# Down projection of an encoder's FFN: seven block products in place of eight, activation operands split ahead and kept in DRAM

## Chip, cores and metric

One core of one Trainium2 chip runs the whole layer in one launch. The metric is device time in microseconds, from launch to the last instruction; three runs of the kernel before took 1522.60, 1526.57 and 1527.08 us. Engines are named as the profile names them: PE is TensorE (PEld its weight loads), DVE is VectorE, ACT is ScalarE, POOL is GpSimd, SP is SyncE.

## What is computed

One layer of a bidirectional encoder over 1024 tokens of width 1024, in float32. The token mixer (a convolution branch and a gated spatial branch, merged) ends in a residual sum; then comes the FFN with DFF = 2816, and a last RMSNorm. The change lies in the FFN:

```python
D_FF = ((8 * D_MODEL // 3 + 255) // 256) * 256      # 2816
h2 = rmsnorm(x, norm_ffn[l])
x = x + (jax.nn.silu(h2 @ w_ffn_gate[l]) * (h2 @ w_ffn_up[l])) @ w_ffn_down[l]
return rmsnorm(x, norm_final)
```

## The kernel before

**Precision.** Every large product is made of three matmuls. An operand is split into a rounded half `hi` (type fp32r, written by ACT, line 84) and the remainder `lo` (DVE, line 85); hi·hi, hi·lo and lo·hi are summed in PSUM. One matmul has 128x128 weights (the stationary operand, loaded by PEld) and 512 moving columns.

**Order of the work.** The program is written with a tile framework. It tracks which instruction writes and reads each tile, sets the semaphores, and picks each engine's fixed order of instructions from its own estimate of when each is ready. So a filler matmul can stand between two blocks that wait for another engine. A PSUM tile of two banks counts as one: a write to one half waits for a read of the other.

**Gate and up (lines 562 to 701).** The 22 row blocks f of DFF go in pairs, f = 2, 4, ..., 20 (0 and 1 are done in the plain way, `plain`, line 564). For a pair, `blocks` (line 653) forms the 2x2 block product of weights and activations with seven products instead of eight; they are numbered 1, 2, 6, 5, 7, 3, 4 in the order in which they run. A product is `block`, 12 matmuls. Sums of weight blocks are made and split in `w_operands` (line 610). Products accumulate into the PSUM halves b1, b2 (tile pa) and b3 (tile pb); between them ACT copies a partial sum out (lines 662, 666, 668) and DVE subtracts it (lines 664, 670, 672). First the gate's seven products run, then the up's; DVE multiplies the two, line 693 and, for the block that ends last, line 696. The product, a tile pair `fa`, is written to DRAM tensors `ff_d` by a DMA that POOL issues (line 700).

**Down (lines 704 to 771).** The output is 8 token tiles of 128 by 1024 columns. It is made in two halves h of four token tiles, each with its four full PSUM tiles. For each of 22 f, SP loads the half's activations (`load_ff`, 256 KB, split into hi and lo) and the weight rows (`load_wd`, 512 KB, split; the last twelve f are kept split for the second half). Per f and token tile run 3 x 2 matmuls, two column halves with the same weights in PE:

```python
for l, r in ((lh, wh), (lh, wl), (ll, wh)):
    for c in cols:
        nc.tensor.matmul(p[c], l[:, sl], r[:, c * H:(c + 1) * H], ...)
```

The last eight f (from `LAST`) are held back and run tile by tile, so that `finish` (line 723) of one tile runs beside the matmuls of the next: DVE adds the residual (732), ACT squares (733), DVE scales by the norm's weights (739), POOL takes the power (741), DVE and ACT scale (745, 747), SP stores.

**Memory.** Pool `act` has 42 buffers of 4 KB a partition, `ws` (raw weights) 3, `wh` (split weights) 4.

Of the kernel before, what the change touches and what calls it, by code (L numbers as in the profile page):

```python
# [32 lines left out]
def encoder_kernel(ctx, tc, x, w_in, w_v, vecs, w_conv_out, sgu_b, w_sp, b_sp,  # L33
                   w_sgu_out, w_o, w_gate, w_up, w_down, norm_final, out):
    nc = tc.nc
# [211 lines left out]
    wg = wnext(0)  # L247
# [7 lines left out]
    pg, pv = PS("pg_0"), PS("pv_0")  # L255
# [249 lines left out]
    def two(name, dt=F32):  # L505
        return A(name, dt, (P, 2, H))
# [52 lines left out]
            h2_transpose(0, (2, 3))  # L559


    ff_d = [dram.tile([P, S], F32, name=f"ff_d{f}") for f in range(NF)]

    def plain(p, w, h):

# [21 lines left out]
    h2_transpose(1, (2, 3))  # L587
    plain(pg, wg, 1)
    plain(pu, wu, 1)
    glu_pair(0, pg, pu)  # L590
    wg = wnext()
    pg = PS("fg_1")
    for h in range(2):
# [6 lines left out]
        plain(pu, wu, h)  # L600
    h2_sums(2)
    h2_sums(3)
    glu_pair(1, pg, pu)

    def w_raw(src, name):
        w = wp.tile([P, D], F32, tag="ws", name=f"ws_{name}", bufs=3)
        nc.sync.dma_start(w, src)
        return w

    def w_operands(src, f, name):  # L610


        r0, r1 = w_raw(src[f], f"{name}{f}"), w_raw(src[f + 1], f"{name}{f + 1}")
        x11, x12, x21, x22 = r0[:, :H], r0[:, H:], r1[:, :H], r1[:, H:]
        sa, sb = two(f"sa_{name}{f}"), two(f"sb_{name}{f}")
        sp, sq, sr, sz = sa[:, 0, :], sa[:, 1, :], sb[:, 0, :], sb[:, 1, :]
        out = {}

        def put(n, s):
            if n in (6, 7, 3):  # L620
                o = two(f"w{n}_{name}{f}", F32R)
            else:
                o = wp.tile([P, 2, H], F32R, tag="wh", name=f"w{n}_{name}{f}", bufs=4)
# [18 lines left out]
        return out  # L642
# [33 lines left out]
    def ffn_in(f, wg, next_w):  # L676
        a = [two(f"fa_{f + n}") for n in range(2)]

        def gate_block(n, h):
            def put(add):  # L680
                add(a[n][:, h, :])
                nc.scalar.activation(a[n][:, h, :], a[n][:, h, :], AF.Silu)
            return put
        blocks(wg, f"g{f}", gate_block(0, 0),
               lambda b: nc.scalar.activation(a[1][:, 0, :], b, AF.Silu),
               gate_block(1, 1), gate_block(0, 1))
        wu = w_operands(w_up, f, "u")
        u = T(f"u_{f}", (P, 2, H))

        def up_block(n, h, i):  # L690
            def put(add):
                add(u[:, i, :])
                nc.vector.tensor_mul(a[n][:, h, :], a[n][:, h, :], u[:, i, :])
            return put
        blocks(wu, f"u{f}", up_block(0, 0, 0),
               lambda b: nc.vector.tensor_mul(a[1][:, 0, :], a[1][:, 0, :], b),
               up_block(1, 1, 1), up_block(0, 1, 0))
        wn = next_w()
        for n in range(2):
            nc.gpsimd.dma_start(ff_d[f + n], a[n].rearrange("p a b -> p (a b)"))  # L700
        return wn


    KEEP = 10
    LAST = 14
    kept = {}

    def load_wd(f):
        if f in kept:
            return kept[f]  # L710
        w = load_split(w_down[f * P:(f + 1) * P, :], f"d{f}", pool=act if f >= KEEP else None)
# [11 lines left out]
    def finish(t, p):

        x2 = A(f"x2b_{t}")
        nc.gpsimd.dma_start(x2, x2_d[t])
        o = A(f"o_{t}")
        ss = small.tile([P, 2], F32, tag="ss2", name=f"ss2_{t}")
        v = small.tile([P, 1], F32, tag="ms", name=f"ms_f{t}")
        for c in range(2):  # L730
            cs = slice(c * H, (c + 1) * H)
            nc.vector.tensor_add(x2[:, cs], x2[:, cs], p[c])  # L732
            nc.scalar.activation(o[:, cs], x2[:, cs], AF.Square, scale=D ** -0.5,
                                 accum_out=ss[:, c:c + 1])
            if c == 0:
                nc.vector.tensor_scalar(ss[:, 0:1], ss[:, 0:1], EPS, None, ALU.add)
            else:
                nc.vector.tensor_add(v, ss[:, 1:2], ss[:, 0:1])
            nc.vector.tensor_mul(x2[:, cs], x2[:, cs], nf[:, cs])
        r = small.tile([P, 1], F32, tag="rstd", name=f"rstd_f{t}")  # L740
        nc.gpsimd.tensor_tensor(r, v, nhalf[:, 0:1], op=ALU.pow)
        for c in range(2):
            cs = slice(c * H, (c + 1) * H)
            if c == 0:
                nc.vector.tensor_scalar(o[:, cs], x2[:, cs], r, None, ALU.mult)
            else:
                nc.scalar.activation(o[:, cs], x2[:, cs], AF.Copy, scale=r)
            nc.sync.dma_start(out[t * P:(t + 1) * P, cs], o[:, cs])

    wg = w_operands(w_gate, 2, "g")  # L750
    for f in range(2, NF, 2):
        wg = ffn_in(f, wg, lambda: w_operands(w_gate, f + 2, "g") if f + 2 < NF else None)

    nf = A("nf_bc")
    nc.gpsimd.dma_start(nf, norm_final.to_broadcast([P, D]))
    for h in range(2):
        p = [PS(f"fd_{4 * h + t}") for t in range(4)]
        tail = {}
        for f in range(NF):
            ffs, wd = load_ff(f, h), load_wd(f)  # L760
            if f >= LAST:
                tail[f] = ffs, wd
                continue
            for t in range(4):
                tm_mm(halves(p[t]), ffs, wd, slice(t * P, (t + 1) * P), f == 0, False)
        for t in range(4):
            for c in range(2):
                for f, (ffs, wd) in tail.items():
                    tm_mm(halves(p[t]), ffs, wd, slice(t * P, (t + 1) * P), False,
                          f == NF - 1, (c,))  # L770
            finish(4 * h + t, halves(p[t]))
# [60 lines left out]
```

## Time and profile before

| | us |
|---|---|
| median of three runs (lowest to highest) | 1526.57 (1522.60 to 1527.08) |
| the profiled execution's own time | 1524.07 |
| its span, first to last instruction | 1522.3 |
| PE busy | 1497.1 |
| DVE busy | 901.1 |
| ACT busy | 441.5 |
| POOL busy | 68.0 |

The span is cut by the views into stretches: the mixer until about 835, gate and up until 1270, the down projection until 1512, and the end. A busy PE says that a matmul was in it; whether PE ran without a hole is told by the chain of waits and by what the engines waited for. Granted clock 1.00 means 2.4 GHz.

### The profile page before, as it was taken

What the parts mean: (1) busy time and instruction counts of PE and PEld (TensorE: products, weight loads), DVE (VectorE), ACT (ScalarE), POOL (GpSimd) and SP (SyncE); (2) the same over time, 40 slices, a digit from 0 to 9 for tenths busy, and PEclk for the clock granted to TensorE, in tenths of its full rate; (3) what the DMA queues carried; (4) which work ended last, traced back from release to release, by engine and by line L of the source; (5) the groups of instructions that cost most, each with busy time, mean ns of one, the idle gap of its engine ahead of it and who ended that gap; (6) DMA issues with size and microseconds to landing.
All of it is one profiled execution on the core that took longest, in us unless ns stands there. A gap on an engine that the chain in (4) does not pass through costs nothing.

```text
span 1522.3 us, 16449 instructions
## 1 busy us (share of the span) xinstructions
PE 1497.1 (98%) x6728; PEld 1233.7 (81%) x6728; DVE 901.1 (59%) x1075; ACT 441.5 (29%) x643; POOL 68.0 (4%) x116
## 2 busy tenths in 40 slices
PE   6999999999999999999999999999999999999997
PEld 6888898888888888888888888888888888887885
DVE  4789699578999815633623665555555554443402
ACT  5221001111111113821313543333333333332401
POOL 1000100000000000010010000000000000000000
PEclk9999999999999999999999999999999999999999
DMA  4250001111112222371431122222222225753402
GB/s 184 59 163 14 1 28 50 47 55 43 58 67 78 75 77 90 110 277 43 152 139 70 56 69 84 84 83 84 84 83 83 81 93 186 223 179 119 172 2 81
DMA packets 43035, 141.73 MB, mean 93 GB/s; under 512 B 4784, under 2 KB 4784, under 8 KB 42960
## 3 DMA queue, kind: packets, MB, share of 16 engines
q1 hardware_dynamic: 32256, 101.73, 20.9%
q0 software_dynamic: 10704, 38.96, 7.1%
q8 instruction: 52, 0.85, 0.2%
q14 instruction: 23, 0.19, 0.0%
HBM read 112.36 MB, written 28.31 MB: 92 GB/s over the span
## 4 chain that ended last, share of the span: by engine, by line
PE 98%; DVE 0%; DMA 0%; ACT 0%; issue 0%; POOL 0%; POOLq 0%; SPq 0%; DVEq 0%; ACTq 0%
PE fd L494 16%; PE pa_u L649 9%; PE pa_g L649 9%; PE pga L110 6%; PE po L494 6%; PE pco L110 6%; PE py L110 6%; PE pb L110 6%; PE pu L110 6%; PE pg L110 6%; PE pv L110 6%; PE pb_u L649 4%; PE pb_g L649 4%; PE v L300 2%; PE v L298 2%; PE v L299 2%
## 5 line engine op out<-in xcount | busy, mean ns | idle before, releaser
L218 DVE SCALAR_TENSOR_TENSOR conv<-c,vec,conv 128x1021 f32<-128x1021 f32 (+14 forms) x240 | 301.3, 1274 | 4.4
L494 PE MATMUL fd<-wh_d,ff 128*128 128x512 f32 x704 | 199.0, 389 | 2.0 <-ACT ff L84 2.0
L494 PEld LDWEIGHTS fd<-wh_d,ff 128*128 128x128 f32 x704 | 132.0, 188 | 29.9 <-ACT ff L84 2.5
L84 ACT CAST wh_in<-ws_in 128x1024 fp32r<-128x1024 f32 x40 | 42.2, 1054 | 303.3 <-PE pg L110 77.5
L494 PE MATMUL fd<-wl_d,ff 128*128 128x512 f32 x352 | 118.8, 389 | 0.0
L649 PE MATMUL pa_g<-t,w_g 128*128 128x512 f32 x360 | 88.7, 395 | 0.0
L649 PE MATMUL pa_u<-t,w_u 128*128 128x512 f32 x360 | 88.7, 395 | 0.0
L649 PEld LDWEIGHTS pa_u<-t,w_u 128*128 128x128 f32 x360 | 66.0, 188 | 18.2 <-DVE u L664 3.1
L649 PEld LDWEIGHTS pa_g<-t,w_g 128*128 128x128 f32 x360 | 66.0, 188 | 18.2 <-DVE fa L664 3.0
L110 PE MATMUL pg<-hT,wh_in 128*128 128x512 f32 (+1 forms) x272 | 75.2, 388 | 3.1 <-ACT hT L180 1.6
L494 PEld LDWEIGHTS fd<-wl_d,ff 128*128 128x128 f32 x352 | 66.1, 188 | 13.7
L85 DVE TENSOR_TENSOR wl_in<-ws_in,wh_in 128x1024 fp32r<-128x1024 f32 x40 | 48.8, 1220 | 41.2 <-ACT wh_in L84 41.1
L110 PE MATMUL pv<-hT,wh_in 128*128 128x512 f32 (+1 forms) x272 | 70.9, 377 | 0.0
L110 PE MATMUL pga<-hT,wh_in 128*128 128x512 f32 x256 | 69.4, 393 | 0.0
L494 PE MATMUL po<-wh_o,mT 128*128 128x512 f32 x256 | 69.1, 390 | 0.0
L110 PE MATMUL pu<-hT,wh_in 128*128 128x512 f32 x256 | 68.4, 389 | 0.0
L110 PE MATMUL py<-gT,wh_so 128*128 128x512 f32 x256 | 68.4, 389 | 0.0
L110 PE MATMUL pco<-sT,wh_co 128*128 128x512 f32 x256 | 68.4, 389 | 0.0
L110 PE MATMUL pb<-hT,wh_in 128*128 128x512 f32 x256 | 68.4, 389 | 0.0
L85 DVE TENSOR_TENSOR wl_d<-ws_d,wh_d 128x1024 fp32r<-128x1024 f32 x32 | 39.1, 1225 | 45.3 <-ACT wh_d L84 45.2
L110 PEld LDWEIGHTS pg<-hT,wh_in 128*128 128x128 f32 x272 | 51.4, 192 | 14.3 <-ACT hT L180 2.4
L732 DVE TENSOR_TENSOR x2b<-x2b,fd 128x512 f32<-128x512 f32 x16 | 10.3, 684 | 82.5 <-PE fd L494 82.5
(220 smaller groups left out, 2697.2 us busy)
## 6 DMA issues: line engine op xcount, KB each, us to landing
ws_in<-in_w_in SPq DMA_DIRECT2D x40, 512.0 KB, 3.7
ws_d<-in_w_down SPq DMA_DIRECT2D x32, 512.0 KB, 4.3
ws_g<-in_w_gate SPq DMA_DIRECT2D x22, 512.0 KB, 3.8
ws_u<-in_w_up SPq DMA_DIRECT2D x22, 512.0 KB, 3.9
ff_d<-fa POOLq DMA_DIRECT2D x22, 512.0 KB, 4.1
ffr<-ff_d SPq DMA_DIRECT2D x44, 256.0 KB, 3.7
x<-in_x SPq DMA_DIRECT2D x16, 512.0 KB, 6.6
ws_v<-in_w_v SPq DMA_DIRECT2D x8, 512.0 KB, 3.8
```

Of the source, the lines that this page charges most:

```text
L84: nc.scalar.copy(hi, src)
L85: nc.vector.tensor_sub(lo, src, hi.bitcast(F32))
L110: nc.tensor.matmul(p[:, h * H + lo_t:h * H + hi_t], wt[:, sl], a[part][h][j][:, i, lo_t:hi_t], start=(k == 0 and wt is hi and part == 0), ...
L218: nc.vector.scalar_tensor_tensor(o[:, a:b], c[:, a + d:b + d], vcol(V_CW, j * TAPS + t), o[:, a:b], ALU.mult, ALU.add)
L298: nc.tensor.matmul(p[:, i2, :], lh, whi, start=(k == 0), stop=False)
L299: nc.tensor.matmul(p[:, i2, :], lh, wlo, start=False, stop=False)
L300: nc.tensor.matmul(p[:, i2, :], ll, whi, start=False, stop=(k == KT - 1))
L494: nc.tensor.matmul(p[c], l[:, sl], r[:, c * H:(c + 1) * H], start=(start and l is lh and r is wh), stop=(stop and l is ll))
L649: nc.tensor.matmul(p, w[n][:, q, sl], a[i][:, r, :], start=(start and i == 0 and m == 0), stop=(i == 3 and m == 2), skip_group_check=True)
L732: nc.vector.tensor_add(x2[:, cs], x2[:, cs], p[c])
```

## The change

- The down projection too becomes a 2x2 block product with seven products. Blocks: the contraction rows 2i and 2i+1 (i = 0 to 10, `NI` = 11), the token halves, and the two column halves of 512. Each product n runs over the 11 i; one step (n, i) is four token tiles by three matmuls. A product's four results lie in two PSUM tiles (`group`).
- The activation operands: blocks 1, 2, 4 of `fa` go to DRAM raw and are split after loading, as before. The four sums (6, 5, 7, 3) are made by DVE beside gate and up, split there (`ff_out`: four adds, four ACT casts, four subtractions for each pair) and written to DRAM as hi and lo together, 512 KB each. POOL issues these stores, and in the down projection the loads, whose destination has type fp32r.
- The weight sums are made in place in the raw tiles `rlo` and `rhi`, and each of 77 weight operands is split just before use (`down_split`). Loads are issued up to five steps ahead of the running one (`LOADS`), splits two steps (`SPLITS`).
- Residual sums, squares and scales are spread over products 7, 3 and 4; four token tiles are stored during product 4 (DMAs issued by ACT), four after it, the last five i being held back (`LAST`).
- `ws` has 6 buffers instead of 3, the norm's weights are loaded before gate and up, and the space that is kept for POOL's DMA descriptors is 4096 bytes a partition.

```diff
-        ws = wp.tile([P, D], F32, tag="ws", name=f"ws_{name}", bufs=3)
+        ws = wp.tile([P, D], F32, tag="ws", name=f"ws_{name}", bufs=6)
...
+    def ff_out(i, a):
+        x11, x21, x12, x22 = a[0][:, 0, :], a[0][:, 1, :], a[1][:, 0, :], a[1][:, 1, :]
+        for n, blk in ((1, x11), (2, x12), (4, x22)):
+            nc.gpsimd.dma_start(ff_d[n][i], blk)
+
+        o = {n: wp.tile([P, 2, H], F32, tag="ws", name=f"ffo{n}_{i}", bufs=6) for n in (5, 6, 7, 3)}
+        nc.vector.tensor_add(o[5][:, 1, :], x21, x22)
+        nc.vector.tensor_add(o[6][:, 1, :], x11, o[5][:, 1, :])
+        nc.vector.tensor_add(o[7][:, 1, :], x11, x21)
+        nc.vector.tensor_add(o[3][:, 1, :], x12, o[6][:, 1, :])
+        for n in (6, 5, 7, 3):
+            hi, lo = o[n][:, 0, :], o[n][:, 1, :]
+            nc.scalar.copy(hi.bitcast(F32R), lo)
+            nc.vector.tensor_sub(lo, lo, hi)
+            nc.gpsimd.dma_start(ffo_d[n][i], o[n])
...
         wn = next_w()
-        for n in range(2):
-            nc.gpsimd.dma_start(ff_d[f + n], a[n].rearrange("p a b -> p (a b)"))
+        ff_out(f // 2, a)
...
+    LAST, LOADS, SPLITS = 6, 6, 2
+    steps = [(n, i) for n in (1, 2, 6, 5, 7, 3, 4) for i in range(NI)]
...
+        if n in ff_d:
+            raw = wp.tile([P, H], F32, tag="ws", name=f"ffr{n}_{i}", bufs=6)
+            nc.sync.dma_start(raw, ff_d[n][i])
+            raws[n, i] = raw
+        else:
+            fos[n, i] = wp.tile([P, 2, H], F32R, tag="ws", name=f"fo{n}_{i}", bufs=6)
+            nc.gpsimd.dma_start(fos[n, i], ffo_d[n][i])
...
+    def down_mm(p, t, ops, start, stop):
+        a, w = ops
+        sl = slice(t * P, (t + 1) * P)
+        for m, (q, r) in enumerate(((0, 0), (0, 1), (1, 0))):
+            nc.tensor.matmul(p, a[:, q, sl], w[:, r, :], start=(start and m == 0),
+                             stop=(stop and m == 2), skip_group_check=True)
...
+    g1 = group("a")
+    down(1, g1, True)
+    g2 = group("b")
+    down(2, g2, True, copies(s1, g1))
+    down(6, g1, False, [lambda t=t, g=g2: nc.vector.tensor_sub(s1[t], g[t], s1[t])
+                        for t in range(4)])
+    g2 = group("c")
+    down(5, g2, True, copies(s2, g1))
+    down(7, g1, False, copies(s5, g2) + [
+        lambda: get_res(range(4, 8)), lambda: less_res(range(4, 8), 1, s5),
+        lambda: get_res(range(4)), lambda: less_res(range(4), 1, s2),
+        lambda: add_res(range(4), 0, s1)])
+    down(3, g2, False, [lambda t=t: add_res([4 + t], 1, [g1[t]]) for t in range(4)])
+    tail = []
+    for i in range(NI):
+        ops = down_operands(4, i)
+        if i < 4:
+            add_res([i], 1, [g2[i]], last=True)
+        elif i < 8:
+            store(i - 4, nc.scalar, 1)
+        if i >= LAST:
+            tail.append(ops)
+            continue
+        for t in range(4):
+            down_mm(g1[t], t, ops, False, False)
+    for t in range(4):
+        for n, ops in enumerate(tail):
+            down_mm(g1[t], t, ops, False, n == len(tail) - 1)
+        add_res([4 + t], 0, [g1[t]], last=True)
+        store(4 + t, nc.sync, 0)
...
+    nc = _bacc.Bacc("TRN2", target_bir_lowering=False, num_devices=1,
+                     dynamic_dma_scratch_size=4096)
```

**Places where the order moves.** First the PE's order in the down projection. Before, for one f and the first two of four token tiles (fd is the tile's PSUM, wh_d and wl_d the split weight rows, ff the split activations; x2 are the two column halves):

```order
L494 MATMUL fd_8354<-wh_d_8365,ff_0_8360 128x512 x2
L494 MATMUL fd_8354<-wl_d_8366,ff_0_8360 128x512 x2
L494 MATMUL fd_8354<-wh_d_8365,ff_0_8360 128x512 x2
L494 MATMUL fd_8355<-wh_d_8365,ff_0_8360 128x512 x2
L494 MATMUL fd_8355<-wl_d_8366,ff_0_8360 128x512 x2
L494 MATMUL fd_8355<-wh_d_8365,ff_0_8360 128x512 x2
```

With the change, the first three steps of product 1 (fd_a: its two PSUM tiles, two token tiles in each; wd and fo: the split operands of the step):

```order
L811 MATMUL fd_a_8682<-wd_0_8644,fo_0_8641 128x512 x6
L811 MATMUL fd_a_8683<-wd_0_8644,fo_0_8641 128x512 x6
L811 MATMUL fd_a_8682<-wd_1_8650,fo_1_8647 128x512 x6
L811 MATMUL fd_a_8683<-wd_1_8650,fo_1_8647 128x512 x6
L811 MATMUL fd_a_8682<-wd_2_8691,fo_2_8688 128x512 x6
L811 MATMUL fd_a_8683<-wd_2_8691,fo_2_8688 128x512 x6
```

A pair of f was 48 matmuls in each token half; a step is 12, and there are 77 steps.

Second, DVE at the start of a pair's gate products, here f = 18. Before, from the last product of the pair before to the subtraction that PE waits for (line 664: fa from pa and ACT's copy s):

```order
L693 TENSOR_TENSOR fa_7331<-fa_7331,u_7462 128x512
L696 TENSOR_TENSOR fa_7332<-fa_7332,pa_u_7463 128x512
L85 TENSOR_TENSOR w_g_7589<-ws_g_7563,w_g_7589 128x512
L627 SCALAR_TENSOR_TENSOR w_u_7700<-ws_u_7694,w_u_7700 128x512
L664 TENSOR_TENSOR fa_7594<-pa_g_7596,s_g_7598 128x512
```

With the change (ffo: the sums of the pair before; line 724 is 696 before, 567 is 627, 690 is 664):

```order
L584 TENSOR_TENSOR ffo_8_8083<-fa_7819,fa_7820 128x512
L724 TENSOR_TENSOR fa_7820<-fa_7820,pa_u_7951 128x512
L85 TENSOR_TENSOR w_g_8077<-ws_g_8051,w_g_8077 128x512
L585 TENSOR_TENSOR ffo_8_8084<-fa_7819,ffo_8_8083 128x512
L586 TENSOR_TENSOR ffo_8_8085<-fa_7819 128x512
L587 TENSOR_TENSOR ffo_8_8086<-fa_7820,ffo_8_8084 128x512
L591 TENSOR_TENSOR ffo_8_8083<-ffo_8_8083 128x512
L591 TENSOR_TENSOR ffo_8_8084<-ffo_8_8084 128x512
L591 TENSOR_TENSOR ffo_8_8085<-ffo_8_8085 128x512
L591 TENSOR_TENSOR ffo_8_8086<-ffo_8_8086 128x512
L567 SCALAR_TENSOR_TENSOR w_u_8209<-ws_u_8203,w_u_8209 128x512
L690 TENSOR_TENSOR fa_8103<-pa_g_8105,s_g_8107 128x512
```

The eight new operations of the pair before stand ahead of line 690 (once line 664).

Third, PE between product 1 and product 6 of the same gate. Before (pb: product 5, taken forward as a filler; pa with y: product 2; pa with t: product 6):

```order
L649 MATMUL pb_g_7597<-t_0_5609,w_g_7578 128x512 x3
L649 MATMUL pb_g_7597<-t_1_5627,w_g_7578 128x512
L649 MATMUL pa_g_7596<-y_0_5181,w_g_7570 128x512 x3
L649 MATMUL pa_g_7596<-y_1_5185,w_g_7570 128x512 x3
L649 MATMUL pa_g_7596<-y_2_5199,w_g_7570 128x512 x3
L649 MATMUL pa_g_7596<-y_3_5203,w_g_7570 128x512 x3
L649 MATMUL pb_g_7597<-t_1_5627,w_g_7578 128x512 x2
L649 MATMUL pb_g_7597<-t_2_5694,w_g_7578 128x512 x2
L649 MATMUL pa_g_7596<-t_0_5603,w_g_7575 128x512 x3
```

With the change:

```order
L675 MATMUL pb_g_8106<-t_0_5663,w_g_8066 128x512 x3
L675 MATMUL pb_g_8106<-t_1_5681,w_g_8066 128x512 x2
L675 MATMUL pa_g_8105<-y_0_5181,w_g_8058 128x512 x3
L675 MATMUL pa_g_8105<-y_1_5185,w_g_8058 128x512 x3
L675 MATMUL pa_g_8105<-y_2_5199,w_g_8058 128x512 x3
L675 MATMUL pa_g_8105<-y_3_5203,w_g_8058 128x512 x3
L675 MATMUL pb_g_8106<-t_1_5681,w_g_8066 128x512
L675 MATMUL pb_g_8106<-t_2_5748,w_g_8066 128x512 x3
L675 MATMUL pb_g_8106<-t_3_5766,w_g_8066 128x512 x2
L675 MATMUL pa_g_8105<-t_0_5657,w_g_8063 128x512 x3
```

Five fillers instead of four stand ahead of product 2, and six instead of four ahead of product 6.

## Rows read from the trace of the kernel before

**Rows 1.** The page: busy time of each engine, and the chain by engine.

```profile
PE 1497.1 (98%) x6728; PEld 1233.7 (81%) x6728; DVE 901.1 (59%) x1075; ACT 441.5 (29%) x643; POOL 68.0 (4%) x116
...
PE 98%; DVE 0%; DMA 0%; ACT 0%; issue 0%; POOL 0%; POOLq 0%; SPq 0%; DVEq 0%; ACTq 0%
```

**Rows 2.** What PE waited for, whole span: us in total, times, longest.

```profile
PE fd L494 <- ACT ff L84: 2.0, 1, 2.0
```

**Rows 3.** The chain of waits from 1240 us on: start, us, what.

```profile
1270.21 119.69 PE fd L494 x528
...
1391.93 120.03 PE fd L494 x528
...
1511.98 0.70 DVE x2b L732
...
1512.70 0.73 ACT o L733 x2
...
1514.12 0.16 DVE ms_f L738
```

**Rows 4.** Stretches: gate and up, down's two halves, its busiest DMA time.

```profile
core 0: us, PE busy (x) PEld busy (x) DVE busy (x) ACT busy (x) POOL busy (x), PEclk, DMA share, GB/s
882.81:1270.21 387.40, 387.40 (x1681) 310.68 (x1681) 205.50 (x318) 141.96 (x241) 11.16 (x21) 1.00 0.26 85
1270.21:1389.90 119.69, 119.68 (x528) 98.75 (x527) 51.42 (x65) 40.54 (x57) 5.19 (x8) 1.00 0.59 187
1391.93:1511.98 120.05, 120.01 (x528) 98.99 (x528) 34.80 (x56) 28.46 (x47) 5.85 (x8) 1.00 0.30 101
1300.00:1340.00 40.00, 40.00 (x178) 33.14 (x177) 21.25 (x22) 18.27 (x22) 1.07 (x2) 1.00 0.78 243
```

**Rows 5.** Instructions by line from 780 us on: busy us, mean ns | idle before, releaser.

```profile
L85 DVE TENSOR_TENSOR ff<-ffr,ff 128x512 fp32r<-128x512 f32 x44 | 29.8, 689 | 25.7 <-ACT ff L84 25.7
...
L84 ACT CAST ff<-ffr 128x512 fp32r<-128x512 f32 x44 | 27.1, 620 | 37.8 <-DMA ffr<-ff_d 37.5
...
L739 DVE TENSOR_TENSOR x2b<-x2b,nf_bc 128x512 f32<-128x512 f32 x16 | 10.9, 684 | 0.0
...
L637 DVE TENSOR_TENSOR sb_g<-ws_g,ws_g 128x512 f32<-128x512 f32 x10 | 6.9, 686 | 0.0
```

**Rows 6.** Timeline of one pair's gate start (f = 6): start, us, what [idle before].

```profile
960.33 0.69 DVE L696 TENSOR_TENSOR fa<-fa,pa_u 128x512 f32<-128x512 f32 x1 [0.81 <-PE pa_u L649]
...
963.05 0.59 ACT L662 COPY s_g<-pa_g 128x512 f32<-128x512 f32 x1 [2.05 <-PE pa_g L649]
...
963.69 2.59 PEld L649 LDWEIGHTS pa_g<-y,w_g 128*128 128x128 f32 x12 [0.19 <-ACT s_g L662]
...
966.75 0.69 DVE L664 TENSOR_TENSOR fa<-pa_g,s_g 128x512 f32<-128x512 f32 x1 [1.85 <-PE pa_g L649]
...
967.49 2.62 PEld L649 LDWEIGHTS pa_g<-t,w_g 128*128 128x128 f32 x12 [0.30 <-DVE fa L664]
```

**Rows 7.** DMA issues: count, KB each, median us to landing; then sa's spread.

```profile
ff_d<-fa POOLq DMA_DIRECT2D x22, 512.0 KB, 4.1
ffr<-ff_d SPq DMA_DIRECT2D x44, 256.0 KB, 3.7
...
sa<-sa_d POOLq DMA_DIRECT2D x8, 512.0 KB, 8.7
...
x2b<-x_d POOLq DMA_DIRECT2D x8, 512.0 KB, 4.7
...
DMA to landing us min/median/max: 6.4/8.7/12.2
```

**Rows 8.** POOL's own time for a DMA, gate and up, then down.

```profile
L700 POOL DMA_DIRECT2D ff_d<-fa x20 | 10.6, 531 | 366.2 <-DVE fa L693 356.4 <-DVE fa L696 9.8
...
L726 POOL DMA_DIRECT2D x2b<-x_d x8 | 4.9, 609 | 83.4 <-PE fd L494 83.4
```

More of the change, by code (lines that the diff above doesn't have):

```diff
@@ L559, in encoder_kernel, with split_to, split_neg @@
             h2_transpose(0, (2, 3))
-    ff_d = [dram.tile([P, S], F32, name=f"ff_d{f}") for f in range(NF)]
+    def split_to(s, o):
+        split(s, o[:, 0, :], o[:, 1, :])
+    def split_neg(s, o):
+        nc.scalar.activation(o[:, 0, :], s, AF.Copy, scale=-1.0)
+        nc.vector.scalar_tensor_tensor(o[:, 1, :], s, -1.0, o[:, 0, :].bitcast(F32),
+                                       ALU.mult, ALU.subtract)
+    NI = NF // 2
+    ff_d = {n: [dram.tile([P, H], F32, name=f"ff_d{n}_{i}") for i in range(NI)] for n in (1, 2, 4)}
+    ffo_d = {n: [dram.tile([P, 2, H], F32, name=f"ffo_d{n}_{i}") for i in range(NI)]
+             for n in (6, 5, 7, 3)}
+    def ff_out(i, a):
[12 more added lines that the diff above has]
+            nc.gpsimd.dma_start(ffo_d[n][i], o[n])
     def plain(p, w, h):
@@ L723, in finish @@
[L723 to L728, printed above, removed]
-        v = small.tile([P, 1], F32, tag="ms", name=f"ms_f{t}")
[L730 to L739, printed above, removed]
+        ff_out(f // 2, a)
@@ new lines, in down_split @@
+    def down_split(n, i):
+        if n in ff_d:
+            a = two(f"fo{n}_{i}", F32R)
+            (split_neg if n == 1 else split_to)(raws.pop((n, i)), a)
+        else:
+            a = fos.pop((n, i))
+        w = two(f"wd{n}_{i}", F32R) if n == 4 and i >= LAST else \
+            wp.tile([P, 2, H], F32R, tag="wh", name=f"wd{n}_{i}", bufs=4)
+        lo, hi = rlo[i], rhi[i]
+        if n == 1:
+            split_to(lo[:, :H], w)
+        elif n == 2:
+            split_to(hi[:, :H], w)
+            nc.vector.tensor_sub(lo[:, :H], lo[:, :H], lo[:, H:])
+        elif n == 6:
+            t2 = A(f"t2_{i}", F32, (P, H))
+            nc.vector.tensor_add(t2, hi[:, H:], lo[:, :H])
+            nc.vector.tensor_sub(hi[:, :H], hi[:, :H], t2)
+            split_to(t2, w)
+        elif n == 5:
+            split_to(lo[:, :H], w)
+        elif n == 7:
+            nc.vector.tensor_sub(lo[:, H:], lo[:, H:], hi[:, H:])
+            split_to(lo[:, H:], w)
+        elif n == 3:
+            split_to(hi[:, H:], w)
+        else:
+            split_to(hi[:, :H], w)
+        ready[n, i] = a, w
@@ new lines, in advance, with down_operands @@
+    def advance(s):
+        for q, (ahead, fn) in enumerate(((LOADS, down_load), (SPLITS, down_split))):
+            while issued[q] < min(len(steps), s + ahead):
+                fn(*steps[issued[q]])
+                issued[q] += 1
+    def down_operands(n, i):
+        advance(steps.index((n, i)) + 1)
+        return ready.pop((n, i))
+    nf = A("nf_bc")
+    nc.gpsimd.dma_start(nf, norm_final.to_broadcast([P, D]))
+    wg = w_operands(w_gate, 2, "g")
+    for f in range(2, NF, 2):
+        wg = ffn_in(f, wg, lambda: w_operands(w_gate, f + 2, "g") if f + 2 < NF else advance(0))
@@ new lines, in down_mm, with down @@
+    def down_mm(p, t, ops, start, stop):
[4 more added lines that the diff above has]
+                             stop=(stop and m == 2), skip_group_check=True)
+    def down(n, p, start, beside=()):
+        for i in range(NI):
+            ops = down_operands(n, i)
+            for t in range(4):
+                down_mm(p[t], t, ops, start and i == 0, i == NI - 1)
+            if i < len(beside):
+                beside[i]()
@@ new lines, in group, with four, get_res @@
+    def group(name):
+        g = [PS(f"fd_{name}{q}", (P, 2, H)) for q in range(2)]
+        return [g[t // 2][:, t % 2, :] for t in range(4)]
+    def four(name):
+        g = [two(f"{name}{q}") for q in range(2)]
+        return [g[t // 2][:, t % 2, :] for t in range(4)]
+    res, ss_t, outs = [None] * 8, [None] * 8, [None] * 8
+    def get_res(ts):
+        for t in ts:
+            res[t] = A(f"x2b_{t}")
+            nc.sync.dma_start(res[t], x2_d[t])
+            ss_t[t] = small.tile([P, 2], F32, tag="ss2", name=f"ss2_{t}", bufs=8)
@@ new lines, in less_res, with add_res @@
+    def less_res(ts, c, less):
+        cs = slice(c * H, (c + 1) * H)
+        for n, t in enumerate(ts):
+            nc.vector.tensor_sub(res[t][:, cs], res[t][:, cs], less[n])
+    def add_res(ts, c, src, last=False):
+        cs = slice(c * H, (c + 1) * H)
+        for n, t in enumerate(ts):
+            nc.vector.tensor_add(res[t][:, cs], res[t][:, cs], src[n])
+        for t in ts:
+            junk = A(f"sq_{t}_{c}", F32, (P, H))
+            nc.scalar.activation(junk, res[t][:, cs], AF.Square, scale=D ** -0.5,
+                                 accum_out=ss_t[t][:, c:c + 1])
+        for t in ts:
+            if last:
+                outs[t] = A(f"o_{t}")
+            nc.vector.tensor_mul((outs if last else res)[t][:, cs], res[t][:, cs], nf[:, cs])
@@ L740, in finish, with store @@
+    def store(t, queue, last):
+        o = outs[t]
+        v = small.tile([P, 1], F32, tag="ms", name=f"ms_f{t}")
         r = small.tile([P, 1], F32, tag="rstd", name=f"rstd_f{t}")
+        nc.vector.scalar_tensor_tensor(v, ss_t[t][:, 0:1], EPS, ss_t[t][:, 1:2], ALU.add, ALU.add)
         nc.gpsimd.tensor_tensor(r, v, nhalf[:, 0:1], op=ALU.pow)
@@ L743, in finish @@
             cs = slice(c * H, (c + 1) * H)
+            src = (o if c == last else res[t])[:, cs]
             if c == 0:
-                nc.vector.tensor_scalar(o[:, cs], x2[:, cs], r, None, ALU.mult)
+                nc.vector.tensor_scalar(o[:, cs], src, r, None, ALU.mult)
             else:
[L747 to L765, printed above, removed]
-        for t in range(4):
[L767 to L771, printed above, removed]
+                nc.scalar.activation(o[:, cs], src, AF.Copy, scale=r)
@@ new lines, in store, with copies @@
+            queue.dma_start(out[t * P:(t + 1) * P, cs], o[:, cs])
+    s1, s2, s5 = four("s1"), four("s2"), four("s5")
+    def copies(d, g):
+        return [lambda t=t: nc.scalar.copy(d[t], g[t]) for t in range(4)]
+    g1 = group("a")
[6 more added lines that the diff above has]
+    down(5, g2, True, copies(s2, g1))
@@ new lines, in encoder_kernel @@
+    down(7, g1, False, copies(s5, g2) + [
[4 more added lines that the diff above has]
+    tail = []
+    for i in range(NI):
+        ops = down_operands(4, i)
[6 more added lines that the diff above has]
+            continue
+        for t in range(4):
+            down_mm(g1[t], t, ops, False, False)
```

50 lines of the change are left out of this document (23 added, 27 removed).

## Prediction

> **What bounds the kernel now.** I read the page first. PE is busy for 1497.1 of 1522.3 us, and 98% of the chain that ended last is PE [rows 1]. So the time is the number of matmuls times their pitch, plus the holes between them; work of DVE, ACT, POOL and the DMAs counts only where PE waits for it. Next I looked at what PE waited for: after the start of the kernel there is one wait of note, 2.0 us for the first split activations of the second token half [rows 2]. The chain shows the same hole from the other side: 528 matmuls from 1270.21 us for 119.69 us, and the next 528 only from 1391.93 us, 2.0 us after the first ended [rows 3]. The pitch in the down projection is 119.69 / 528 = 0.2267 us, and the granted clock is 1.00, so the 2.4 GHz level, throughout [rows 3, 4]. Gate and up run without a real hole too [rows 4]: PE is busy for all of their 387.4 us.
>
> The other engines have room. In gate and up DVE is busy 205.5 of 387.4 us, ACT 142 [rows 4]. In the down projection DVE has 86.2 us in 240 us, ACT 69 us [rows 4]. The DMA engines were busiest from 1300 to 1340 us, at a share of 0.78 for 243 GB/s [rows 4]; PE didn't wait there.
>
> **What the change removes.** The down projection had 22 f x 2 halves x 4 tiles x 6 = 1056 matmuls. It will have 7 products x 11 steps x 4 tiles x 3 = 924. Shape and columns stay, and each matmul had its own weight load already (PEld's count in a half is 528 like PE's [rows 4]), so the pitch stays: 132 x 0.2267 = **29.9 us less**. The hole of 2.0 us lies at the second half's start, when its operands were made only after the first half; the seven products run on without such a restart, their operands being split two steps ahead: **2.0 us less**. At the end, the last tile had both column halves to finish; now one half was done before. From PE's end to the sum of squares stand 2.14 us [rows 3]: one add of 0.70, a square of 0.73, and then the second half's rest until DVE's `ms_f` at 1514.12. With one half the sum can start at 1511.98 + 0.70 + 0.73, some 0.7 us sooner: **0.7 us less**. What follows is as before.
>
> **What it adds beside gate and up.** Each pair gets eight DVE operations on 128x512 (0.69 us each [rows 5]) and four casts (0.62 us [rows 5]): 5.5 us more DVE and 2.5 us more ACT in a pair's 38.7 us, over 20.5 and 14.2 us before. The room is there; what counts is the place. Seven of the eight stand behind DVE's last product of a pair (line 724) and ahead of line 690, for which PE waits before product 6. In the trace DVE was idle for 1.85 us there, started at 966.75 us, and PE's weight load still waited 0.30 us [rows 6]. Now DVE has, from the end of its first operation at 961.02 us, a weight remainder, three adds, four subtractions and a weight remainder: nine operations of 0.69 are 6.2 us, and line 690 ends at 961.02 + 6.2 + 0.69 = 967.9 us. PE by then has product 1, five fillers, product 2 and six fillers, 35 x 0.2267 = 7.9 us from about 960.3, so until 968.2 us. It fits by 0.3 us, since the order has two more fillers there. I take 0. Below: five fillers cover ACT's copy better than four, which left PEld idle for 0.19 us, and the 0.30 us goes as well [rows 6]: at most 0.5 us x 10 pairs = 5 us gained. Above: if each of the four subtractions also waited out its cast, 4 x 0.62 - 0.3 = 2.2 us in nine pairs, 20 us. The casts run on ACT while DVE makes the next sum, so I stay at 0.
>
> **What it adds in the down projection.** A step is 12 x 0.2267 = 2.72 us on PE. DVE has two remainders in a step of product 1 (1.4 us), three operations in products 2 and 6 (2.07 us), at most two later; with residual work 206 operations or some 140 us in 209.5. ACT has some 94 us. Both fit, hidden behind PE with two to three steps of lead. At the start DVE makes the last pair's sums too: about 14 operations, 9.7 us, until the weights of the fifth step, which PE needs after four steps, 10.9 us. That fits narrowly; I take 0.5 us, between 0 and 5. At the end, DVE has about 18 us and ACT as much from the end of product 3 to the last split, and PE comes to it after some 20.9 us: 0.5 us, between 0 and 3.
>
> The loads: products 2 and 6 need 768 KB a step, 289 GB/s, the others 256 to 512 KB. That is more than the 243 GB/s at a share of 0.78, which at a share of 1 would be 311 GB/s [rows 4]. But weight halves are loaded ahead, and over products 1, 2 and 6 it is 23.1 MB in 90 us, 257 GB/s, after a start some 16 us ahead. A sum's load is issued five steps, 13.6 us, before its use. In the mixer POOL's loads of the same 512 KB took 8.7 us to land, 12.2 at most [rows 7]. So I take 0.
>
> What no row shows is a DMA that casts, as these 44 loads do, and one with a quarter of the descriptor space. The nearest rows are POOL's plain 512 KB transfers, 4.1 to 8.7 us to land [rows 7], several of them in flight at once. I take their behaviour. The lower bound is 0, since a hidden load can't gain; the upper is one load at a time (below).
>
> POOL's own time for a DMA is 0.53 us beside gate and up and 0.61 us in the down projection [rows 8], with DVE about half busy in both. The Trainium skill says in "SBUF — State Buffer", section "A bandwidth-pool intuition that's wrong (but worth ruling out)", that a DMA issued by GpSimd which takes about 620 ns alone took about 3100 ns beside a DVE copy that held the shared port. By that figure an estimate of 44 x (3.1 - 2.72) = 17 us would come on top; by the rows nothing does, and the sum goes by the rows.
>
> **Sum.** 1522.3 - 29.9 - 2.0 - 0.7 + 0.5 + 0.5 = 1490.7 us of span. The profiled execution's own time lies 1.8 us above its span, so 1492.5; it is 2.5 us under the median of the three runs, against which the same 31.6 us give 1495. I predict **1494 us**.
>
> **Rivals.**
> *One load at a time (ends slower).* If the sums' loads run one after another, because the cast or the smaller descriptor space lets no second one in, each step of products 6, 5, 7 and 3 takes a load's time instead of 2.72 us. It decides from 3.42 us a load: 44 x (3.42 - 2.72) = 31 us eats the gain. With the 4.1 us of POOL's stores it is 44 x 1.38 = 61 us, 1555 us; with 4.7 us, 1581 us [rows 7]. For it: nothing here has cast in a DMA. Against it: sa and yb landed 8.7 us after issue although both went out within a few us, so POOL's queue holds more than one. 9%.
> *The DMA engines become the bound.* If products 2 and 6 get only the 243 GB/s seen, their 22 steps take 3.24 us each, 22 x 0.52 = 11 us more: 1505 us. Against it stands the lead. 13%.
> *Line 690 comes late.* The 2.2 us in nine pairs of above: 1514 us, or any part of it. 5%.
> *POOL issues only while DVE is idle.* In product 6 DVE's three to four operations, 2.07 to 2.76 us, plus POOL's 0.61 are 2.68 to 3.37 us a step: four steps fall behind by 0.65 us each, 2.6 us, of which the lead hides most; 1497 us at worst. This is the mechanism of the page above; both rows of POOL at 0.53 to 0.61 us speak against it. 3%.
>
> **How the numbers follow.** My case has 70%, 1489 to 1499 us by its bounds. With the DMA rival the range goes to 1505, and I carry it to 1510 for parts of line 690's; below, 1488 for a gain from the fillers. Left out are the slow rival and the far ends. About 0.3% of the time, 4.6 us, is what a measurement of this kernel can tell from no change. All cases but the first rival are faster by more; that one is mostly slower, and for loads of 3.3 to 3.5 us equal. So faster 91%, same 2%, slower 7%.
>
> **What would show it.** Right: 924 matmuls on line 811 over some 210 us, PE's waits in them under 2 us in sum, a pair of gate and up still 38.7 us or a little less. Wrong: PE waiting for a DMA into `fo` (first rival, steps of over 3.4 us in products 6, 5, 7, 3 but not in 1, 2, 4), for `ffr` or `wd` in products 2 and 6 (second), or for line 690 with over 1 us a pair (third); POOL's DMA instructions of 2 us and more (fourth). A time over 1510 us would make the prediction wrong.

## Result, and the profile after

The changed kernel took 1490.35 us (median of 4 runs, 1489.25 to 1492.0) against 1526.63: a ratio of 0.9769, 95% interval 0.9749 to 0.9789. The profiled execution took 1489.25 us with a span of 1487.5. The prediction was 1494 us in a range of 1488 to 1510.

The page has PE busy for all but 20 us of the span (25 before), with 132 matmuls fewer; DVE, ACT and POOL gained work. These lines answer to [rows 1]:

```profile
PE 1467.1 (99%) x6596; PEld 1208.1 (81%) x6596; DVE 989.2 (66%) x1245; ACT 474.1 (32%) x733; POOL 115.1 (8%) x207
```

The chain of waits from 1255 us on (start, us, what) answers to [rows 3]. Where two halves of 528 matmuls stood with 2.0 us between them, six products of 132 follow one another without a hole; the seventh is broken near its end:

```profile
1269.44 29.92 PE fd_a L811 x132
1299.36 29.92 PE fd_b L811 x132
...
1448.96 26.48 PE fd_a L811 x116
...
1475.45 1.28 DVE x2b L848 x2
...
1478.46 0.49 DVE o L868
...
1482.87 0.72 ACT o L870
```

What PE waited for (us, times, longest) answers to [rows 2], and what its weight loads waited for in gate and up to [rows 6]:

```profile
PE fd_a L811 <- DVE x2b L848: 1.2, 1, 1.2
...
PE pa_g L675 <- ACT s_g L688: 0.3, 1, 0.3
```

```profile
PEld pa_g L675 <- ACT s_g L688: 4.0, 10, 0.7
PEld pa_u L675 <- DVE u L690: 3.1, 10, 0.4
```

and in the kernel before, in gate:

```profile
PEld pa_g L649 <- DVE fa L664: 3.0, 10, 0.3
PEld pa_g L649 <- ACT s_g L662: 1.9, 10, 0.2
```

The 2.0 us for split activations are gone; 1.2 us for a residual add at the end are new. In gate, line 690 no longer appears as something that PE waits for (in up it does, as before); ACT's copy on line 688 is waited for longer, 4.0 us for 1.9.

The stretches answer to [rows 4]: gate and up, down from its first matmul to the last token tile's add, and two pieces in which the DMA engines were full:

```profile
880.58:1269.44 388.86, 388.60 (x1681) 311.59 (x1681) 253.98 (x400) 163.77 (x286) 38.17 (x71) 1.00 0.41 143
1269.44:1480.57 211.13, 209.94 (x924) 172.97 (x923) 129.18 (x216) 82.67 (x154) 30.80 (x56) 1.00 0.69 221
1290.00:1320.00 30.00, 30.00 (x134) 24.86 (x133) 26.13 (x45) 13.44 (x24) 3.18 (x6) 1.00 1.00 346
1306.00:1312.00 6.00, 6.00 (x28) 4.99 (x27) 5.37 (x10) 2.81 (x5) 3.15 (x6) 1.00 1.03 356
```

The engines that move data were full for 30 us (share 1.00, 346 GB/s), and PE was busy in all of them.

**Where the 34.8 us of span went**, from the starts of matmuls in the traces, in us (each stretch runs from one matmul's start to another's, the last column from the last matmul's start to the end). The first row and the fifth are the two kernels' profiles shown here and before; the others are of the experiments below.

| run | span | first gate matmul | gate and up | down, first to last matmul | after the last matmul |
|---|---|---|---|---|---|
| before | 1522.3 | 882.6 | 387.4 | 241.5 | 10.7 |
| before, again | 1520.2 | 880.5 | 387.4 | 241.5 | 10.7 |
| before, descriptor space 4096 | 1517.3 | 880.5 | 387.4 | 241.5 | 7.9 |
| before, that and six buffers | 1518.3 | 880.3 | 387.4 | 242.7 | 7.9 |
| after | 1487.5 | 880.4 | 388.9 | 210.9 | 7.3 |
| after, again | 1488.8 | 882.6 | 387.8 | 210.8 | 7.6 |
| three load slots | 1491.6 | 880.5 | 388.0 | 215.5 | 7.6 |
| two load slots | 1539.9 | 882.6 | 387.7 | 261.5 | 8.1 |
| splits in down | 1486.2 | 880.6 | 387.7 | 210.8 | 7.0 |
| tail order | 1484.7 | 880.5 | 387.7 | 209.2 | 7.3 |
| cast 7 on DVE | 1486.0 | 880.5 | 387.4 | 210.8 | 7.3 |
| tail order and cast 7 | 1486.5 | 882.3 | 387.7 | 209.2 | 7.3 |

Down gave 30.6 us. The rest (2.2 in front of gate, 3.4 at the end, 1.5 lost in gate and up) I had not forecast in this way, so the first experiments were on it.

### The profile page after: what moved, and what is told of

Read it like the earlier page. It is cut to its first block, busy times and chain, and to the rows that moved or that the text cites. A ratio compares the mean times of both kernels' runs of the same rounds, so it can differ in the third digit from the quotient of the medians.

```text
span 1487.5 us, 16766 instructions
## 1 busy us (share of the span) xinstructions
PE 1467.1 (99%) x6596; PEld 1208.1 (81%) x6596; DVE 989.2 (66%) x1245; ACT 474.1 (32%) x733; POOL 115.1 (8%) x207
## 4 chain that ended last, share of the span: by engine, by line
PE 97%; DVE 1%; issue 0%; ACT 0%; DMA 0%; POOL 0%; SPq 0%; POOLq 0%; ACTq 0%; DVEq 0%
PE pa_u L675 9%; PE pa_g L675 9%; PE fd_a L811 8%; PE pga L110 6%; PE po L494 6%; PE pco L110 6%; PE py L110 6%; PE pb L110 6%; PE pu L110 6%; PE pv L110 6%; PE pg L110 6%; PE fd_c L811 4%; PE pb_u L675 4%; PE pb_g L675 4%; PE fd_b L811 2%; PE v L299 2%
## 5 line engine op out<-in xcount | busy, mean ns | idle before, releaser
L811 PE MATMUL fd_a<-wd,fo 128*128 128x512 f32 x528 | 120.8, 390 | 1.2 <-DVE x2b L848 1.2
L811 PEld LDWEIGHTS fd_a<-wd,fo 128*128 128x128 f32 x528 | 99.0, 188 | 22.4 <-DVE x2b L848 1.9
L85 DVE TENSOR_TENSOR wd<-wd,wd 128x512 fp32r<-128x512 f32 x66 | 45.2, 687 | 53.5 <-ACT wd L84 53.5
L84 ACT CAST wd<-wd 128x512 fp32r<-128x512 f32 x66 | 40.8, 621 | 73.6 <-PE fd_c L811 33.3
L675 PE MATMUL pa_u<-y,w_u 128*128 128x512 f32 x240 | 60.3, 393 | 0.0
L811 PE MATMUL fd_c<-wd,fo 128*128 128x512 f32 x264 | 60.2, 389 | 0.0
```

Of the source, the lines that this page charges most:

```text
L675: nc.tensor.matmul(p, w[n][:, q, sl], a[i][:, r, :], start=(start and i == 0 and m == 0), stop=(i == 3 and m == 2), skip_group_check=True)
L811: nc.tensor.matmul(p, a[:, q, sl], w[:, r, :], start=(start and m == 0), stop=(stop and m == 2), skip_group_check=True)
```

## Experiments

**1. How much differs between executions.** Both kernels, unaltered, profiled a second time.

> The changed kernel once more, unaltered. Theory S (the 2.2 us that went in front of gate and up come from the change, by its six load buffers or its descriptor space): gate's first matmul again at 880.6 us of the span, within 0.5, and the ratio to the kernel before within 0.001 of 0.977. Rival V (they are a difference between executions): gate's first matmul anywhere from 880 to 884, and the whole span moves with it. In both the down projection takes 211 us from its first matmul to the last token tile's add, with one PE wait of 1.2 us in front of its end.

> The kernel before, unaltered, for a second profile of it. If the 3.0 us at the end of the program and the granted clock of 0.94 to 0.97 in the first 38 us belong to this kernel, both are there again, and gate starts near 882.7 us; if they are the execution's, one or both are gone and gate starts near 880.4.

Measured: 1489.85 us for the changed kernel (5 runs, ratio 0.9773, 0.976 to 0.9787), 1521.95 us in one run for the kernel before. Gate begins at 882.6 us in this profile of the changed kernel and at 880.5 in this one of the kernel before, the other way round from the first two: rival V holds. The stretches of both profiles of the kernel before, first one, then again, show what differs; the last three numbers are granted clock, DMA share and GB/s:

```profile
17.00:19.00 2.00, 1.55 (x8) 1.10 (x8) 2.00 (x6) 2.00 (x5) 0.00 (x0) 0.92 0.54 213
19.00:21.00 2.00, 2.00 (x12) 2.00 (x11) 1.70 (x4) 1.12 (x3) 0.00 (x0) 0.50 0.00 0
21.00:23.00 2.00, 2.00 (x15) 2.00 (x13) 0.72 (x3) 0.81 (x2) 0.00 (x0) 0.73 0.63 145
```

```profile
17.00:19.00 2.00, 1.71 (x12) 1.34 (x11) 1.69 (x6) 2.00 (x5) 0.00 (x0) 1.00 0.61 244
19.00:21.00 2.00, 1.51 (x12) 1.13 (x10) 2.00 (x4) 1.48 (x4) 0.00 (x0) 1.00 0.00 0
21.00:23.00 2.00, 2.00 (x16) 1.85 (x16) 0.92 (x3) 2.00 (x5) 0.55 (x1) 1.00 0.89 250
```

In the execution with the late gate PE ran at a granted clock of 0.50, the 1.2 GHz level, from 19 to 21 us, having been busy 1.55 of the 2 us before and waiting for operands in the rest; in the other the clock stayed at 1.00. All four profiles that begin gate after 882 us have a mean clock of 0.93 to 0.96 from 20 to 38 us, all eight others 1.00. The two profiles of the kernel before are 2.1 us apart by 27 us, and keep that distance until gate; that the clock is the whole of it isn't shown. So the 2.2 us in front of gate are not the change's. Of the 1.5 us lost in gate and up, 1.1 are not either: the same instructions took 388.9 us once and 387.8 the second time. The 10.7 us at the end of the kernel before, however, are there in both of its profiles.

**2. The end of the program.** The change also sets `dynamic_dma_scratch_size=4096` and six load buffers for three. Both alone in the kernel before, then the first by itself:

```
+                     dynamic_dma_scratch_size=4096)
...
-        ws = wp.tile([P, D], F32, tag="ws", name=f"ws_{name}", bufs=3)
+        ws = wp.tile([P, D], F32, tag="ws", name=f"ws_{name}", bufs=6)
```

> The kernel before with nothing but six load buffers for three and the smaller descriptor space. Theory S: gate's first matmul at 880.6 us for 882.8, the ratio to the kernel before 0.9985, and of the change's 35 us only 33 belong to the seven products. Rival V: gate's first matmul at 882 to 884 in the profiled execution and a ratio of 1.000 within 0.001. A third outcome, slower (ratio over 1.001), would mean that the smaller descriptor space costs something that the seven products pay back.

> The kernel before with the smaller descriptor space alone, three load buffers as before. Theory B (the six buffers are what moved the kernel before to a ratio of 0.9984): ratio 1.000 within 0.001, DMA rate of the first 20 us near 323 GB/s as before, not 360. Rival D (the descriptor space): ratio 0.9984 again, and the 3.0 us that SyncE waits for TensorE's sequencer at the end of the program fall to 0.5 as they did with both edits.

Measured: both edits 1521.31 us and a ratio of 0.9984 (0.9975 to 0.9993); descriptor space alone 1519.62 us and again 0.9984 (0.9975 to 0.9993). Theory S's numbers came out (gate at 880.3 us, 0.9984), but not its mechanism: gate begins there in the unaltered kernel too (experiment 1). Theory B fell: the buffers gain nothing (they do raise the first 20 us from 323 to 364 GB/s, but gate begins where it did, and down took 1.2 us more in that profile), the descriptor space does all. The waits of SyncE's queue at the end (us, times, longest) and the drains of POOL's queue (ns min/median/max, first and last start), in the kernel before:

```profile
SPq L828 <- PEq L828: 3.5, 2, 3.0
SPq L828 <- DMA out<-o: 1.4, 2, 0.8
```

```profile
L828 POOLq DRAIN  x3: 40/93/7106, 1514.4 to 1522.0; - x3
```

and with the smaller descriptor space:

```profile
SPq L829 <- DMA out<-o: 1.4, 2, 0.8
SPq L829 <- PEq L829: 0.7, 2, 0.5
```

```profile
L829 POOLq DRAIN  x3: 40/102/1957, 1512.3 to 1517.0; - x3
```

The program ends with a drain on each engine. POOL's began at 1514.4 us, as its last operation began, and took 7.1 us, until 1521.5; the last store had landed by 1518.6, when SyncE's queue reached its own first drain. With the smaller space the drain took 1.96 us and ended before the stores did. The view names PE's queue as what SyncE waited for; the row of drains shows that the one still running was POOL's. That is 2.8 us at the end, of which the change keeps 2.3 net. From the start of the last scaling to the end 6.95 us became 4.6, counted from line 747 before and from line 870 in the chain above; its drain takes 2.2 us and is over before the last store lands:

```profile
1515.32 0.72 ACT o L747
```

```profile
L965 POOLq DRAIN  x3: 46/93/2222, 1482.2 to 1487.1; - x3
```

**3. Are the sums' loads hidden by their lead alone?** Slots of the load buffers are held by tiles that nothing else uses (three or four), so that three or two stay in use:

```
+    hold = [wp.tile([P, D], F32, tag="ws", name=f"hold{n}", bufs=6) for n in range(4)]
+    for h in hold:
+        nc.gpsimd.memset(h[:, 0:8], 1.0)
...
+    for h in hold:
+        nc.gpsimd.tensor_tensor(h[:, 0:1], h[:, 0:1], outs[7][:, 0:1], op=ALU.pow)
```

The last two lines stand behind the last store and keep the slots taken until then.

> The changed kernel with four of the six load slots held through the down projection by tiles that nothing uses, so that two are left. Theory (the cast loads are hidden by their lead and nothing else): a load issues when the step two before it ends, lands 4.5 us later, and the steps between take 2.72; two steps then take 4.5 + 2.72 = 7.2 us for 5.4, which is 0.9 us a step, 40 us over the 44 steps of products 6, 5, 7 and 3, and TensorE's waits name the fo loads. Rival (transfers this size come at the DMA engines' rate, and slots beyond two only hold data): down rises by under 10 us, and in products 1 and 2 alone, where the engines were full.

> The changed kernel with three of its six load slots held through the down projection, so that three are left. Theory (a load is hidden as long as it lands within the steps that the other slots bridge): with three slots a load issues two steps, 5.4 us, ahead of its use and lands in 4.5 us or less where the engines are not full, so that products 5, 7 and 3 wait for nothing; only where product 6's loads run beside those of down's weights, and landed in up to 9.4 us, does TensorE wait, 2 to 10 us in all against the 51 us that two slots cost. Rival (every slot taken away costs in proportion): half of the way from six slots to two, some 25 to 38 us, with waits in all four products.

Measured, one run each: two slots 1541.67 us, down 261.5 us, 50.7 more; three slots 1493.33 us, down 215.5 us, 4.6 more. With two, PE waits for the loads by name (us, times, longest), and POOL's issues in the timeline (start, us, [idle before]) come in twos, about every 7.3 us in products 5 and 7, where with six slots they come singly every 2.72:

```profile
PE fd_a L815 <- DMA fo<-ffo_d: 18.1, 13, 3.2
PE fd_c L815 <- DMA fo<-ffo_d: 15.1, 14, 2.6
```

```profile
1401.30 0.53 POOL L757 DMA_DIRECT2D fo<-ffo_d  x1 [3.90 <-PE fd_c L815]
1404.03 0.54 POOL L757 DMA_DIRECT2D fo<-ffo_d  x1 [2.20 <-PE fd_c L815]
1408.74 0.53 POOL L757 DMA_DIRECT2D fo<-ffo_d  x1 [4.18 <-PE fd_c L815]
```

A load issues when PE leaves the slot two steps back, and the pair of steps takes a landing, a step and what lies between. In the chain (start, us, what) one such pair takes 7.5 us:

```profile
1426.04 4.07 DMA fo<-ffo_d
1430.25 3.01 PE fd_a L815 x12
1433.55 4.05 DMA fo<-ffo_d
```

The theory's 7.2 us came out nearly, but by other terms: the landing was shorter (3.8 us in the median for 4.5), the 12 matmuls took 3.0 us to the end of the last for 2.72, and 0.4 us lay between. Products 5 and 7 lost 10.0 and 10.3 us, as forecast (0.9 us a step). The 50.7 us are over the 40 forecast mainly by product 6, which lost 15.7: its pairs took 10 us, their loads landed in up to 7.0 us beside those of down's weights, and after such waits the granted clock was 0.91 on the mean from 1330 to 1370 us. Product 3 lost 12.0 us, and product 4, whose loads take the same slots, 2.7. With three slots PE waits for them twice, in product 6 alone, the longer time for a load that took 8.8 us to land:

```profile
PE fd_a L815 <- DMA fo<-ffo_d: 3.5, 2, 3.0
```

So the price isn't in proportion to the slots. It jumps where the lead falls under a landing: 13.6 us (six slots) and 5.4 us (three) cover the usual landing of 3.8 to 4.5, 2.7 us (two) don't. One load at a time, the prediction's first rival, would have shown in products 6, 5, 7 and 3 with any number of slots.

**4. Did the splits have to be made beside gate and up?** The four sums are stored whole and split in down:

```
...
-            hi, lo = o[n][:, 0, :], o[n][:, 1, :]
-            nc.scalar.copy(hi.bitcast(F32R), lo)
-            nc.vector.tensor_sub(lo, lo, hi)
-            nc.gpsimd.dma_start(ffo_d[n][i], o[n])
+            nc.gpsimd.dma_start(ff_d[n][i], o[n][:, 1, :])
```

> The changed kernel with one part undone: gate and up store the four sums as plain f32, and the down projection loads 256 KB for 512 on SyncE's queue and splits them itself (44 casts of 0.62 us on ScalarE and 44 subtractions of 0.69 us on VectorE move from gate and up to down). Theory (the splits have room in either place, since VectorE would be busy 159 of down's 211 us): down stays at 211 us within 1, gate and up fall to 387.4, and the time is 0 to 1.5 us under the changed kernel's. Rival (the stretch decides, not the mean): VectorE was busy 29.0 of product 2's 29.6 us, splits of product 6 are queued into that stretch, TensorE waits there for operand tiles by 3 to 8 us, and the time rises by that.

Measured: 1489.34 us, ratio 0.9779 (0.9765 to 0.9792), not to be told from the changed kernel. Down took 210.8 us with the same single wait, gate and up 387.7. In product 2's stretch DVE was busy throughout, and PE still was too:

```profile
1298.40:1328.40 30.00, 30.00 (x134) 24.82 (x133) 30.00 (x51) 16.55 (x31) 0.00 (x0) 1.00 0.69 230
```

The rival's wait didn't come. Operands are split two steps ahead, and I put it down to that lead that a stretch in which DVE is full cost nothing; a shorter lead was not tried. The moved splits, and loads of halves ready for PE, are no part of the gain; the seven products are.

**5. The wait at down's end.** PE ran the held-back matmuls of the last four token tiles in the order 0, 2, 1, 3 (15 for each tile; 14 of tile 2's stood ahead of tile 1's, the last one right behind them), DVE added the tiles in the order 0, 1, 2, 3. Tiles 2 and 3 share a PSUM tile, so PE's tile 3 waited for the add of 2, and that stood behind the add of 1.

```
-    for t in range(4):
+    for t in (0, 2, 1, 3):
         for n, ops in enumerate(tail):
```

> The changed kernel with its last four token tiles in the order 0, 2, 1, 3, in which TensorE runs them, so that VectorE adds tile 2 before tile 1. Theory: TensorE's only wait in the down projection (1.2 us, for the add that reads the PSUM tile shared by token tiles 2 and 3) goes, and the span falls from 1487.5 by 1.0 to 1.3 us at the same start of gate. Rival: the wait only moves to the shared tile of 0 and 1, and the span stays within 0.3 us.

Measured: 1487.55 us, ratio 0.9763 (0.975 to 0.9776). No wait for line 848 is left among PE's, and down took 209.2 us for 210.9. The gain in down is 1.6 us rather than 1.0 to 1.3, and no hole is left: from the start of the first to the start of the last of 924 matmuls are 923 times the 0.2267 us of [rows 3], 209.2 us. The span fell by 2.8 us, but 1.2 of them are gate and up, where the two kernels don't differ.

**6. ACT's queue in gate.** In the timeline of the changed kernel two of the new casts run ahead of the copy that PE waits for:

```profile
960.48 1.23 ACT L590 CAST ffo<-ffo 128x512 fp32r<-128x512 f32 x2 [0.84 <-DVE ffo L585]
...
961.61 0.58 ACT L688 COPY s_g<-pa_g 128x512 f32<-128x512 f32 x1
...
962.24 2.63 PEld L675 LDWEIGHTS pa_g<-y,w_g 128*128 128x128 f32 x12 [0.39 <-ACT s_g L688]
```

The cast of operand 7 goes to DVE; then with experiment 5's edit as well:

```
-            nc.scalar.copy(hi.bitcast(F32R), lo)
+            (nc.vector.tensor_copy if n == 7 else nc.scalar.copy)(hi.bitcast(F32R), lo)
```

> The changed kernel with the cast of operand 7 (one of the four beside gate and up) on VectorE for ScalarE, so that two casts and not three stand ahead of ScalarE's copy of the gate product. Theory (the queue on ScalarE is what gate and up lost): that copy is waited for 0.19 us a pair as in the kernel before, a pair takes 38.73 us for 38.88, and gate and up fall from 388.9 to 387.3, about 1.5 us. Rival (VectorE's order is as full as ScalarE's): the cast of 0.7 us takes up VectorE's idle 0.67 us in front of line 690, TensorE waits for that by 0.1 to 0.6 us a pair, and gate and up stay at 389 or rise to 393.

> The changed kernel with both edits: the last four token tiles in the order 0, 2, 1, 3, and the cast of operand 7 on VectorE. Theory (they act in different stages and add up): gate and up at 387.4 us, no wait at down's end, 1.2 us and 0.3 to 1.1 us, together 1.5 to 2.3 us under the changed kernel and a ratio to the kernel before of 0.976 within 0.001. Rival: the ratio stays at 0.977, since the one stage's gain is within what executions differ by.

Measured: 1488.95 us, ratio 0.9773 (0.9759 to 0.9786); with both edits 1488.26 us, 0.9764 (0.9751 to 0.9777). What weight loads waited for in gate with the cast moved:

```profile
PEld pa_g L675 <- DVE fa L690: 2.7, 9, 0.3
PEld pa_g L675 <- ACT s_g L688: 2.1, 10, 0.3
```

The wait for ACT's copy fell from 4.0 to 2.1 us, and the one for line 690 came back with 2.7. Gate and up took 387.4 us, with both edits 387.7; unaltered they took 387.8 in the second profile and 387.7 to 388.0 in those of the lead and of the tail's order. Nothing can be told apart here, so this half is inconclusive. From the first gate matmul to the end both edits took 604.2 us, the tail's order alone 604.2, the changed kernel 607.1 and 606.2. The version to keep is the tail's order: the wait is gone from its profile and its median is the lowest, though its interval still overlaps the changed kernel's, so that the time alone doesn't tell the two apart.

The moved cast shows one thing more. DVE made it in 0.42 us (ACT: 0.62), and in ten of eleven places it met a DMA instruction of POOL that had just begun. That instruction took 0.76 us for 0.54 and ended 0.12 us after the cast, and the run with both edits shows the same:

```profile
1000.84 0.76 POOL L592 DMA_DIRECT2D ffo_d<-ffo  x1 [2.57 <-DVE ffo L591]
1001.07 0.42 DVE L590 CAST ffo<-ffo 128x512 fp32r<-128x512 f32 x1
...
1002.04 0.54 POOL L592 DMA_DIRECT2D ffo_d<-ffo  x1 [0.43 <-issue]
```

## Why the prediction was right, step by step

- **132 matmuls at one pitch, 29.9 us.** Right: six products of 29.92 us each in the chain, the pitch of [rows 3], and the granted clock 1.00 throughout.
- **The hole of 2.0 us.** Right: no restart shows; the first product begins straight behind up's last. Counted from start to start the hole was 2.3 us (241.5 less 1055 times the pitch), and with it down's 30.6 us add up: 29.9 + 2.3 - 1.6, the last being the wait of the next point.
- **Start and end of down, 0.5 us each.** The start cost nothing. The end cost 1.2 us of wait, 1.6 by experiment 5, but not where I put it. I feared late operands; it was a PSUM tile shared by two token tiles and an order of adds that wasn't PE's. That step failed as a mechanism inside the bound of 0 to 3 us.
- **The tail, 0.7 us.** Right for its term: from the last add to `ms_f` 2.14 us became 1.47. But the end got shorter by 3.4, not 0.7. The sentence that failed is "what follows is as before": 2.3 us net came from POOL's drain (experiment 2), which the chain of [rows 3] doesn't reach, since it follows work and not drains. POOL's last operation also took 0.55 us for 0.86, a further 0.4 with its start.
- **Gate and up, 0.** Near: 0.3 to 1.5 us lost, of which executions of the same kernel differ by 1.1; the gain that was to be the lower bound didn't come. Line 690 fitted as worked out (its wait in gate went). "Five fillers cover ACT's copy better" was wrong: I counted the fillers of PE and not the casts that stand ahead of the copy on ACT.
- **Loads, 0.** Right, and for the reason given: the lead, as experiment 3 shows. The rate at a full share was put at 311 GB/s from [rows 4]; it was 346 to 356 in down, and 410 from 17 to 21 us of the same execution, so a share of 1 stands for no single rate.
- **The sum.** 1490.7 us of span forecast, 1487.5 measured: 2.3 of the 3.2 us are the drain, and 2.2 lie in the first 38 us, where executions of either kernel differ by that; gate and up took 1.5 back. Down's own terms were right to 0.3 us (30.9 forecast); that the whole came so near is in part luck, since these three were not in the sum and partly cancel. The median fell by 36.3 us for the 32.6 forecast, and by 33.8 in the second measurement, where the kernel before took 1523.63 us. Of the signs named beforehand, 924 matmuls over 211 us and a wait under 2 us in them came; a pair of gate and up at 38.7 us or a little less didn't, it took 38.8 to 38.9.
- **Rivals.** One load at a time fell: with six slots loads issue every 2.72 us and land after 4.5 (median). The DMA engines were the bound of nothing, though full. Line 690 was not late. POOL's DMA instructions on line 757 took 0.53 us each, the first six of them while DVE was busy 5.37 of 6 us; the 3100 ns that the Trainium skill ("SBUF — State Buffer", "A bandwidth-pool intuition that's wrong (but worth ruling out)") gives beside a DVE copy don't appear, and by this measurement the fourth rival falls for this kernel. DVE made sums and differences there and no copy; beside its cast, in experiment 6, POOL's instruction did get longer, by 0.23 us. (DVE's "about half busy" in the prediction is 53% in gate and up and 36% in the down projection by [rows 4].)

```profile
L757 POOL DMA_DIRECT2D fo<-ffo_d x44 | 23.2, 528 | 132.5 <-PE fd_a L811 66.3 <-PE fd_c L811 35.1 <-DMA ffr<-ff_d 28.7
```

## What to carry to other kernels

Where one engine is busy for 98% of the span, count its instructions first. What is left is here mostly a question of lead, and the number to check is lead (slots less one, times the step) against landing time, not the mean load of a queue or of an engine. Take a change apart into its side edits: here the size of a descriptor space alone gave 2.3 to 2.9 us that would have been put down to the algorithm. And profile both kernels twice before explaining 1 to 2 us: stages that nobody touched moved by that much.

## What the runs showed of the hardware

- The final drain of POOL's queue took 7.1 us with the default descriptor space and 1.96 us with 4096, in a program whose other instructions are the same. No run shows why.
- A load of 512 KB that casts f32 to fp32r landed in 4.5 us (median; 3.5 to 9.4), like POOL's plain stores of that size (4.4).
- The granted clock fell to the 1.2 GHz level for some 3 us near the start in four of the twelve profiles, with the same instructions; what decides it stays open.
- A DMA instruction of POOL that had begun 0.22 us before a cast on DVE (f32 to fp32r, 128x512, 0.42 us) took 0.76 us for 0.54, in 20 of 20 meetings in two profiles. A plain f32 copy on DVE (line 433, 128x1024, 1.22 us) left a DMA instruction within it at 0.53 us, once in the changed kernel's profile.
